# Summing the seven block products of a feed-forward chunk in PSUM instead of on VectorE

## The chip, the core and the metric

The kernel runs on one core of a Trainium2 chip. The metric is the device time of one execution in microseconds (us), as the median of several runs. Of the core's engines the text speaks of TensorE (PE in the profile; its weight loads are PEld), VectorE (DVE), ScalarE (ACT), GpSimd (POOL) and SyncE (SP). SP and POOL issue the DMA transfers that matter here. Matrix products are written to PSUM, which has eight banks of 512 float32 values per partition; DVE and ACT read and write PSUM as well as the main on-chip memory, SBUF.

## The reference: a two-layer decoder trunk

The input `x` is 512 tokens of 1024 channels, float32. Layer 0 mixes tokens by a dilated windowed attention with three head groups, layer 1 by causal pooling over 2, 4, 8 and 16 tokens. Each mixer is followed by the same kind of feed-forward block:

```python
def swiglu_ffn(h, w_gate_up, w_down):
    gu = h @ w_gate_up
    gate, up = gu[..., :D_FF], gu[..., D_FF:]
    return (jax.nn.silu(gate) * up) @ w_down

def reference(x, ...):
    for i in range(DEPTH):            # DEPTH = 2
        x = x + mixer_i(rmsnorm(x, ...))
        x = x + swiglu_ffn(rmsnorm(x, ffn_norm[i]), w_ffn_gate_up[i], w_ffn_down[i])
    return rmsnorm(x, final_norm)
```

`D_FF` is 2816, that is 22 chunks of 128 hidden channels. For one chunk the kernel needs a gate product and an up product of 128 channels each, by 512 tokens, over 1024 input channels.

## The kernel before, in words

**Precision.** Every operand is split into a high part (`hi`, a rounded copy that ACT makes, line 77) and a low part (`lo`, the rest, which DVE makes, line 78). A product is three matmuls, hi by hi, hi by lo and lo by hi, added up in PSUM. The split is done for weights and for activations alike.

**Stages.** Attention comes first (to about 510 us of the span), then layer 0's feed-forward (to about 858), the pooling (to about 918), layer 1's feed-forward, and the final norm in the last few us.

**Order of the feed-forward.** `ffn` handles one layer in two halves of 11 chunks. Chunks 0 to 4 of the first half are done plainly (`plain_pair`): a gate product and an up product of 24 matmuls each with 512 columns. During these, `prepare(k)` builds for k = 0 to 3 the sums and differences of activation blocks, `T`, that the later chunks need. The other 6 chunks of the first half and all 11 of the second go through `strassen_pair`, so there are 17 of them in a layer and 34 in all. After each half come the down products of that half.

**A chunk of seven products.** Gate and up, two halves of the tokens, and two halves of the input channels make a product of 2 by 2 blocks. The kernel forms it from seven block products instead of eight (a Strassen-Winograd scheme). Each block product, `mult`, is 12 matmuls of 256 columns (four k steps of three). `seven` runs them in this order; the weight part (b, s, m or l) and the activation block are in brackets: 11 (b), 21 (b), 1 (s), 3 (s), 2 (m), 22 (m), 4 (l). They go to halves of four PSUM banks, each product into space of its own, and DVE adds them up afterwards: line 412 makes gt from two products and `first`, line 420 makes `sums`, lines 425 and 426 make `up` and the second half of `gt`. ACT copies the first product to SBUF (`first`, line 399), and at the end `activation` does the silu on ACT (line 865), the product of gate and up on DVE (line 866), and the split of the result into hi and lo. The result is written to `act` and feeds the down products. All PSUM tiles come from one ring of eight banks.

**Weights.** A chunk's weights come as `Pair`. `load` issues three DMAs on SP (lines 134, 135 and 136: raw tiles b and a, half tile c) and then one on POOL (line 137), which adds a further block onto b in place while it loads. Four later steps make the split parts: `blocks` (part b, from a), `sums` (part s, from the summed raw tile b), `more` (part m, from a after two additions on DVE, lines 150 and 151) and `last` (part l, from c). The rings are short: five split tiles of type w, two halves, four raw tiles, two raw halves. In program order, `pump` emits the next step as soon as the buffer that it would reuse has been given up (`done()`); `seven` calls `pump` after each product. Counting back five w tiles, part m of the next chunk reuses the tile of part b of this chunk, part b of the chunk after reuses this chunk's s, and part s of the chunk after reuses this chunk's m.

**What sets the order on an engine.** The program is written in one order, but a planner decides, before the kernel runs, the order of the instructions on each engine. It plays the program through with costs of its own and takes, on each engine, the earliest written instruction that is ready at that moment. That order is then fixed. On the chip each engine takes its instructions in it and waits at the first one whose inputs or buffers are not there. Line 77 is the `hi` of a split, line 78 its `lo`, 254, 255 and 257 the matmuls of plain and down products, 371, 372 and 373 those of `mult`.

Of the kernel before, what the change touches and what calls it, by code (L numbers as in the profile page):

```python
# [15 lines left out]
P = 128  # L16
# [32 lines left out]
def trunk(ctx: ExitStack, tc: tile.TileContext, xT, norms, w_first, w_qk, w_qkp, w_v0, w_v0p, w_v12, w_out, w_pair, w_down, w_pin, w_pgrp,  # L49
# [4 lines left out]
    tmp = ctx.enter_context(tc.tile_pool(name="tmp", bufs=2))  # L54
    psum = ctx.enter_context(tc.tile_pool(name="psum", bufs=8, space=PSUM))

# [8 lines left out]

    def ps():
        return psum.tile([P, S], F32, tag="ps", name="ps")

# [157 lines left out]
    class Product:  # L226


        def __init__(self, n, ins, w=None, keep=None):
            self.n, self.ins, self.done, self.p, self.w = n, ins, 0, ps(), w  # L230
            self.sizes = DOWN if n == HALF else (n,)
            self.tiles, self.keep = keep or [], keep is not None
# [133 lines left out]

    def mult(dst, w, half, T, name):
        for k in range(K2):
            c = slice(half * S + k * P, half * S + (k + 1) * P)
            th, tl = T[name, k]  # L370
            nc.tensor.matmul(dst, w.t[0][:, c], th, start=k == 0, stop=False)  # L371
            nc.tensor.matmul(dst, w.t[0][:, c], tl, start=False, stop=False)  # L372
            nc.tensor.matmul(dst, w.t[1][:, c], th, start=False, stop=k == K2 - 1)  # L373

# [53 lines left out]

    def normed(layer, k, row):
# [20 lines left out]

    with tc.tile_pool(name="opool", bufs=1) as opool:
        early = opool.tile([P, HEADS, S], F32R, tag="o", name="early")
# [398 lines left out]

    with tc.tile_pool(name="fpool", bufs=2) as fpool:
        fpool.tile([P, 32], F32, name="shift", bufs=1)
# [9 lines left out]
        def activation(gt, up):  # L863

            nc.scalar.activation(gt, gt, AF.Silu)
            nc.vector.tensor_mul(up, up, gt)
            j = len(act)
            held["a", j], t = slot("a")
            act.append((t[:, 0], t[:, 1]))
            split(*act[-1], up)  # L870

        def unfold(m, p):

            if m == 0:
                held["x", 0], t = slot("xs", F32)
                new = t[:, 0]
            else:
                new = x_tile(m - 1)
            nc.vector.tensor_add(new.rearrange("p (b i r) -> p r i b", r=NT, b=NT), *(
                t.rearrange("p (r i b) -> p r i b", r=NT, b=NT) for t in (X[m], p)))  # L880
            X[m] = new

        def ffn(layer, nxt, lead, row):
# [23 lines left out]
            def prepare(k):  # L907


                h, t = normed(op, k, row)  # L910
                hq, b22 = h.t.rearrange("p (a b c) -> p a b c", a=2, b=2), h.t[:, 3 * H2:]
# [137 lines left out]
        def end(i, half, js, f=None):  # L1049
            f = f or Product(HALF, hidden, keep=ends[i])  # L1050
            return f.add(js, cols=halves[half])

        def add(i, half, f):
            m, cols = KC - 2 + i, halves[half]
            nc.vector.tensor_add(X[m][:, cols], X[m][:, cols], f.p[:, cols])
            sq = ftile("sq", H2)
            nc.scalar.activation(sq, X[m][:, cols], AF.Square)
            return sq
# [106 lines left out]
```

## Time and profile before

| | |
|---|---|
| Timed runs | 1267.69, 1268.29 and 1268.46 us; median 1268.29 us |
| Span of the profiled execution, first to last instruction | 1264.5 us; no other time of that execution is given |
| PE busy | 1250.9 us, 99% of the span |
| DVE busy | 926.3 us, 73% |
| ACT busy | 571.5 us, 45% |
| POOL busy | 130.1 us, 10% |
| Chunks of seven products | 34: starting at 553.7 to 604.4 (6), 674.4 to 775.2 (11), 960.7 to 1011.4 (6) and 1081.3 to 1182.1 us (11) |

The rows of the profile read as follows. A row that groups instructions gives line, engine and operation, then the tiles written and read, the shape, the count, the busy time in us, the mean duration of one in ns, and the idle time of the engine just before these instructions with what ended it. A row of a timeline gives start and duration in us, the engine, the line, and in square brackets the idle time before and its releaser. A row of a stretch gives start and end in us, its length, then the busy time of PE, PEld, DVE, ACT and POOL with the count of instructions, the granted share of the PE clock, the DMA engines' busy share and GB/s. A matmul's duration is longer than the distance to the next one, because matmuls overlap; the distance between starts is what counts.

### The profile page before, as it was taken

The page shows a single profiled execution, that of the slowest core. Times are in us where ns is not written, and L with a number is a line of the kernel's source. Part 1 is how long each engine was busy: PE and PEld are TensorE (multiplying, and loading weights), DVE is VectorE, ACT ScalarE, POOL GpSimd, SP SyncE. Part 2 cuts the span into 40 slices and gives each one's busy share as a digit, 9 for nine tenths or more (in the row PEclk, how much of TensorE's full clock was granted, in tenths as well). Part 3 has the DMA queues.
Part 4 walks back from the last instruction along what each step waited for, and adds up shares of the span by engine and source line. Part 5 has one row for each costly group of instructions (what it writes and reads, how often), then busy time and mean ns, then how long its engine had stood idle before and what let it go on. Part 6 is the DMA issues. An engine that isn't in the chain of part 4 may idle for free.

```text
span 1264.5 us, 21069 instructions
## 1 busy us (share of the span) xinstructions
PE 1250.9 (99%) x8382; PEld 1156.7 (91%) x8382; DVE 926.3 (73%) x1395; ACT 571.5 (45%) x885; POOL 130.1 (10%) x123
## 2 busy tenths in 40 slices
PE   9999999999999999999999999999999999999997
PEld 7889999999999988899989999888789988999987
DVE  6987788878778845689636887558978953788643
ACT  6445554545445543445324554343444532455331
POOL 1011111212111000110001110000301000110000
PEclk9999999999999999999999999999999999999999
DMA  8336556655756433256456774333135645676322
GB/s 295 101 95 164 130 157 145 162 139 144 182 137 152 139 133 120 67 129 181 124 146 158 181 188 126 97 133 130 37 95 123 175 126 142 168 182 173 93 69 67
DMA packets 67875, 174.04 MB, mean 138 GB/s; under 512 B 6960, under 2 KB 9152, under 8 KB 67776
## 3 DMA queue, kind: packets, MB, share of 16 engines
q1 hardware_dynamic: 48816, 136.49, 33.3%
q0 software_dynamic: 17808, 35.14, 16.4%
q8 instruction: 66, 1.08, 0.3%
q10 hardware_dynamic: 1152, 1.05, 0.2%
q14 instruction: 33, 0.27, 0.1%
HBM read 170.56 MB, written 2.10 MB: 137 GB/s over the span
## 4 chain that ended last, share of the span: by engine, by line
PE 75%; issue 12%; DVE 10%; ACT 1%; POOL 1%; DMA 0%; DVEq 0%; POOLq 0%
PE ps L372 13%; PE ps L371 13%; PE ps L373 13%; PE ps L254 8%; PE ps L255 8%; PE ps L257 8%; PE ps L483 2%; PE ps L484 2%; PE ps L485 2%; DVE wlo L78 2%; PE ps L678 1%; PE ps L590 1%; DVE raw L434 1%; POOL rcol L323 1%; PE ps L656 1%
## 5 line engine op out<-in xcount | busy, mean ns | idle before, releaser
L77 ACT ACTIVATE whi<-raw 128x1024 fp32r<-128x1024 f32 (+2 forms) x299 | 298.1, 1002 | 428.2 <-PE ps L255 198.4
L78 DVE TENSOR_TENSOR wlo<-raw,whi 128x1024 fp32r<-128x1024 f32 (+2 forms) x299 | 343.2, 1152 | 158.6 <-ACT whi L77 157.4
L254 PE MATMUL ps<-a,whi 128*128 128x512 f32 (+1 forms) x374 | 141.0, 377 | 0.0
L255 PE MATMUL ps<-a,whi 128*128 128x512 f32 (+1 forms) x374 | 140.9, 377 | 0.0
L257 PE MATMUL ps<-a,wlo 128*128 128x512 f32 (+1 forms) x374 | 140.8, 377 | 0.0
L371 PE MATMUL ps<-tt,whi 128*128 128x256 f32 x408 | 115.5, 283 | 0.0
L372 PE MATMUL ps<-tt,whi 128*128 128x256 f32 x408 | 115.5, 283 | 0.0
L373 PE MATMUL ps<-tt,wlo 128*128 128x256 f32 x408 | 115.5, 283 | 0.0
L137 POOL DMA_DIRECT2D raw<-w_pair x34 | 41.1, 1209 | 440.8 <-DMA raw<-w_pair 152.6
L257 PEld LDWEIGHTS ps<-a,wlo 128*128 128x128 f32 x374 | 70.4, 188 | 13.0
L254 PEld LDWEIGHTS ps<-a,whi 128*128 128x128 f32 x374 | 70.4, 188 | 12.8
L255 PEld LDWEIGHTS ps<-a,whi 128*128 128x128 f32 x374 | 70.4, 188 | 12.7
L371 PEld LDWEIGHTS ps<-tt,whi 128*128 128x128 f32 x408 | 78.3, 192 | 0.0
L372 PEld LDWEIGHTS ps<-tt,whi 128*128 128x128 f32 x408 | 78.3, 192 | 0.0
L373 PEld LDWEIGHTS ps<-tt,wlo 128*128 128x128 f32 x408 | 78.3, 192 | 0.0
L372 PE MATMUL ps<-tb,whi 128*128 128x256 f32 x272 | 77.2, 284 | 0.1
L373 PE MATMUL ps<-tb,wlo 128*128 128x256 f32 x272 | 77.0, 283 | 0.0
L371 PE MATMUL ps<-tb,whi 128*128 128x256 f32 x272 | 76.9, 283 | 0.0
L371 PE MATMUL ps<-h,whi 128*128 128x256 f32 x252 | 72.7, 289 | 0.0
L373 PE MATMUL ps<-h,wlo 128*128 128x256 f32 x252 | 71.3, 283 | 0.0
L372 PE MATMUL ps<-h,whi 128*128 128x256 f32 x252 | 71.3, 283 | 0.0
L254 PE MATMUL ps<-h,whi 128*128 128x512 f32 x144 | 56.4, 392 | 0.0
(280 smaller groups left out, 3415.5 us busy)
## 6 DMA issues: line engine op xcount, KB each, us to landing
raw<-w_pair SPq DMA_DIRECT2D x78, 512.0 KB, 4.3
raw<-w_qkp SPq DMA_DIRECT2D x36, 512.0 KB, 4.7
raw<-w_pair POOLq DMA_DIRECT2D x34, 512.0 KB, 7.2
raw<-w_down SPq DMA_DIRECT2D x32, 384.0 KB, 3.1
raw<-w_down SPq DMA_DIRECT2D x32, 320.0 KB, 2.8
raw<-w_v SPq DMA_DIRECT2D x18, 512.0 KB, 3.9
raw<-w_qkp POOLq DMA_DIRECT2D x18, 512.0 KB, 7.3
rawhalf<-w_pair SPq DMA_DIRECT2D x34, 256.0 KB, 3.5
```

What stands on the lines that cost most here:

```text
L77: nc.scalar.activation(hi, v, AF.Copy)
L78: nc.vector.tensor_tensor(lo, v, hi.bitcast(F32), op=OP.subtract)
L137: nc.gpsimd.dma_start(self.b.t.rearrange("p (a c) -> p a c", a=2), self.src[:, None, 3 * S:].to_broadcast([P, 2, S]), accum_op=OP.add)
L254: nc.tensor.matmul(self.p[:, cols], w[0][:, s], mh[:, cols], start=self.done == 0, stop=False)
L255: nc.tensor.matmul(self.p[:, cols], w[0][:, s], ml[:, cols], start=False, stop=False)
L257: nc.tensor.matmul(self.p[:, cols], w[1][:, s], mh[:, cols], start=False, stop=self.done == self.n)
L371: nc.tensor.matmul(dst, w.t[0][:, c], th, start=k == 0, stop=False)
L372: nc.tensor.matmul(dst, w.t[0][:, c], tl, start=False, stop=False)
L373: nc.tensor.matmul(dst, w.t[1][:, c], th, start=False, stop=k == K2 - 1)
L483: nc.tensor.matmul(o, mh, wh, start=k == 0, stop=False)
L484: nc.tensor.matmul(o, mh, wl, start=False, stop=False)
L485: nc.tensor.matmul(o, ml, wh, start=False, stop=k == K2 - 1)
```

## The change

`strassen_pair` no longer calls `seven`, but a new function, `chain`. The seven products run in another order: 11, 1, 2, 21, 3, 22, 4. Four of them (11, 2, 3, 4) go to the same half bank `c` and add up there, and `c` is read in between:

- after 11, ACT copies `c` to a second bank `d`; after 2, ACT copies `c` to a third bank `e`. Product 21 is then added onto `d`, product 22 onto `e`.
- product 1 has a bank of its own, `a`, and ACT copies it to SBUF (`half`).
- `left`: ACT takes the silu of `d` straight from PSUM into the first half of `gt`. `right`: DVE subtracts `half` from `e`, then ACT takes the silu of that half.
- `high`: DVE subtracts `half` from `c` after product 3 into the second half of `up`. `low`: ACT copies `c` after product 4 into the first half of `up`.

`hide`, the part of `activation` behind the silu, stays: product of gate and up on DVE, then the split. DVE's lines 412, 420, 425 and 426 and ACT's copy `first` are gone from the feed-forward, but not from the attention, which still uses `seven`. The signs are kept right by a flipped sum in `prepare` (`normed(..., flip=True)`), a factor of -1 in the plain chunks' `up`, and a subtraction instead of an addition where the down products are added to `X`. PSUM is no longer one ring of eight in the feed-forward: `c` has 2 banks, `d` and `e` share 3, and `a` and the plain products' ring has 3; whole products alternate between the last two rings.

```diff
+    def banks(stack, **sizes):
+        psum["pool"] = stack.enter_context(tc.tile_pool(name="psum", bufs=1, space=PSUM))
+        psum["sizes"], psum["turn"] = sizes, 0
+
+    def full():
+        tags = [t for t in ("seed", "ps") if t in psum["sizes"]]
+        psum["turn"] += 1
+        return ps(tags[psum["turn"] % len(tags)])
...
-    def mult(dst, w, half, T, name):
+    def mult(dst, w, half, T, name, onto=False):
         for k in range(K2):
             c = slice(half * S + k * P, half * S + (k + 1) * P)
             th, tl = T[name, k]
-            nc.tensor.matmul(dst, w.t[0][:, c], th, start=k == 0, stop=False)
...
+            nc.tensor.matmul(dst, w.t[0][:, c], th, start=k == 0 and not onto, stop=False, skip_group_check=onto)
...
+    def chain(T, share, left, right, low, high):
+        unit, = units.popleft()
+        c, a, d, e = (ps(tag)[:, :H2] for tag in ("sum", "ps", "seed", "seed"))
+        wb = part(unit, "b")
+        mult(c, wb, 0, T, "11")
+        nc.scalar.copy(d, c)
+        pump()
+        ws = part(unit, "s")
+        mult(a, ws, 0, T, "1")
+        share(a)
+        pump()
+        wm = part(unit, "m")
+        mult(c, wm, 0, T, "2", True)
+        nc.scalar.copy(e, c)
+        pump()
+        mult(d, wb, 1, T, "21", True)
+        wb.done()
+        left(d)
+        pump()
+        mult(c, ws, 1, T, "3", True)
+        ws.done()
+        high(c)
+        pump()
+        mult(e, wm, 1, T, "22", True)
+        wm.done()
+        right(e)
+        pump()
+        wl = part(unit, "l")
+        mult(c, wl, 0, T, "4", True)
+        wl.done()
+        low(c)
+        pump()
...
-        nc.vector.tensor_add(t.t[:, 3 * H2:], t.t[:, H2:S], h.t[:, S:3 * H2])
+        if flip:
+            nc.vector.scalar_tensor_tensor(t.t[:, 3 * H2:], t.t[:, H2:S], -1.0, h.t[:, S:3 * H2],
+                                           op0=OP.mult, op1=OP.subtract)
...
+        banks(stack, sum=2, seed=3, ps=3)
...
-                nc.vector.tensor_mul(up, pu, row)
+                nc.vector.scalar_tensor_tensor(up, pu, -1.0, row, op0=OP.mult, op1=OP.mult)
...
             def strassen_pair():
-                gt, up = ftile("gt"), ftile("up")
-                seven(T, gt, up, ftile)
-                activation(gt, up)
+                gt, up, half = ftile("gt"), ftile("up"), ftile("half", H2)
+                lo, hi = slice(0, H2), slice(H2, S)
+
+                def right(p):
+                    nc.vector.tensor_sub(gt[:, hi], p, half)
+                    nc.scalar.activation(gt[:, hi], gt[:, hi], AF.Silu)
+
+                chain(T, lambda p: nc.scalar.copy(half, p),
+                      lambda p: nc.scalar.activation(gt[:, lo], p, AF.Silu), right,
+                      lambda p: nc.scalar.copy(up[:, lo], p),
+                      lambda p: nc.vector.tensor_sub(up[:, hi], p, half))
+                hide(gt, up)
...
-                        nc.vector.tensor_add(X[m], X[m], f.p)
+                        nc.vector.tensor_sub(X[m], X[m], f.p)
...
-            f = f or Product(HALF, hidden, keep=ends[i])
+            f = f or Product(HALF, hidden, keep=ends[i], part=True)
```

More of the change, by code (lines that the diff above doesn't have):

```diff
@@ L54, in trunk @@
     tmp = ctx.enter_context(tc.tile_pool(name="tmp", bufs=2))
-    psum = ctx.enter_context(tc.tile_pool(name="psum", bufs=8, space=PSUM))
+    psum = {}
     def x_tile(k, name="x", dtype=F32):
@@ L64, in trunk, with ps @@
     nhalf = cpool.tile([P, NT], F32, name="nhalf")
[L66 to L67 removed]
+    def ps(tag="ps"):
+        pool, sizes = psum["pool"], psum["sizes"]
+        return pool.tile([P, S], F32, tag=tag, name=tag, bufs=sizes[tag])
+    def banks(stack, **sizes):
[5 more added lines that the diff above has]
+        return ps(tags[psum["turn"] % len(tags)])
     tmp.tile([P, 64], F32, name="shift", bufs=1)
@@ L226, in trunk, with __init__ @@
     class Product:
-        def __init__(self, n, ins, w=None, keep=None):
-            self.n, self.ins, self.done, self.p, self.w = n, ins, 0, ps(), w
+        def __init__(self, n, ins, w=None, keep=None, part=False):
+            self.n, self.ins, self.done, self.w = n, ins, 0, w
+            self.p = ps() if part else full()
             self.sizes = DOWN if n == HALF else (n,)
@@ L370, in mult @@
             th, tl = T[name, k]
-            nc.tensor.matmul(dst, w.t[0][:, c], th, start=k == 0, stop=False)
-            nc.tensor.matmul(dst, w.t[0][:, c], tl, start=False, stop=False)
-            nc.tensor.matmul(dst, w.t[1][:, c], th, start=False, stop=k == K2 - 1)
+            nc.tensor.matmul(dst, w.t[0][:, c], th, start=k == 0 and not onto, stop=False, skip_group_check=onto)
+            nc.tensor.matmul(dst, w.t[0][:, c], tl, start=False, stop=False, skip_group_check=onto)
+            nc.tensor.matmul(dst, w.t[1][:, c], th, start=False, stop=k == K2 - 1, skip_group_check=onto)
     def part(unit, name):
@@ L427, in seven, with normed @@
         behind(6)
-    def normed(layer, k, row):
+    def chain(T, share, left, right, low, high):
[30 more added lines that the diff above has]
+        pump()
+    def normed(layer, k, row, flip=False):
         h, t = Held("raw"), Held("raw")
@@ L448, in in_a_row @@
         return t.rearrange("p (r i b) -> p b i r", b=NT, r=NT)
-    with tc.tile_pool(name="opool", bufs=1) as opool:
+    with tc.tile_pool(name="opool", bufs=1) as opool, ExitStack() as stack:
+        banks(stack, ps=8)
         early = opool.tile([P, HEADS, S], F32R, tag="o", name="early")
@@ L850, in trunk @@
                 note(1, m)
-    with tc.tile_pool(name="fpool", bufs=2) as fpool:
+    with tc.tile_pool(name="fpool", bufs=2) as fpool, ExitStack() as stack:
+        banks(stack, sum=2, seed=3, ps=3)
         fpool.tile([P, 32], F32, name="shift", bufs=1)
@@ L878, in unfold @@
                 new = x_tile(m - 1)
-            nc.vector.tensor_add(new.rearrange("p (b i r) -> p r i b", r=NT, b=NT), *(
+            nc.vector.tensor_sub(new.rearrange("p (b i r) -> p r i b", r=NT, b=NT), *(
                 t.rearrange("p (r i b) -> p r i b", r=NT, b=NT) for t in (X[m], p)))
@@ L907, in prepare @@
             def prepare(k):
-                h, t = normed(op, k, row)
+                h, t = normed(op, k, row, True)
                 hq, b22 = h.t.rearrange("p (a b c) -> p a b c", a=2, b=2), h.t[:, 3 * H2:]
```

6 lines of the change are left out of this document (5 added, 1 removed).

## The prediction

> **What bounds the kernel now.** I read the page first (busy shares and the groups with their idle time), then the four stretches that hold the 34 chunks of seven products, then the waits, and then single timelines inside the chunks.
>
> ```profile
> span 1264.5 us, 21069 instructions
> PE 1250.9 (99%) x8382; PEld 1156.7 (91%) x8382; DVE 926.3 (73%) x1395; ACT 571.5 (45%) x885; POOL 130.1 (10%) x123
> ...
> L371 PE MATMUL ps<-tt,whi 128*128 128x256 f32 x408 | 115.5, 283 | 0.0
> ```
>
> ```profile
> 553.73:614.53 60.80, 60.74 (x506) 60.54 (x505) 53.06 (x77) 31.32 (x46) 4.82 (x4) 1.00 0.66 173
> 674.38:785.26 110.88, 110.88 (x926) 110.87 (x924) 91.60 (x126) 56.20 (x75) 9.66 (x8) 1.00 0.63 166
> 960.69:1021.49 60.80, 60.75 (x506) 60.55 (x505) 52.95 (x77) 31.33 (x46) 4.82 (x4) 1.00 0.64 173
> 1081.33:1192.21 110.88, 110.88 (x926) 110.88 (x925) 90.90 (x125) 55.35 (x74) 9.66 (x8) 1.00 0.61 159
> ```
>
> PE bounds it. The second stretch holds 11 chunks of 84 matmuls in 110.88 us, which is 10.08 us a chunk, 1.44 us a product and 0.12 us a matmul; the fourth is the same to the hundredth. The first and third hold 6 chunks each, 60.48 us at that pace, and take 60.80, so 0.32 us each is lost. That 0.64 us is all the waiting that PE does in the 34 chunks. The change leaves the count and shape of the matmuls alone, so **0.64 us is the most that it can win there**, however much it takes from DVE. What is open is what it loses: today PE runs ahead of DVE and ACT, and from now on it has to wait for them inside a chunk.
>
> How far behind they may be shows here; the last three rows are the second chunk of layer 0's first stretch, from 564.12 on, and the answers below them the second chunk of layer 1's, from 971.06 on.
>
> ```profile
> ACT whi L77 <- DMA raw<-w_pair: 13.1, 5, 5.4
> ```
>
> ```profile
> 563.29 1.06 ACT L77 ACTIVATE whi<-raw 128x1024 fp32r<-128x1024 f32 x1 [1.28 <-DMA raw<-w_pair]
> 568.88 1.06 ACT L77 ACTIVATE whi<-raw 128x1024 fp32r<-128x1024 f32 x1 [4.53 <-DMA raw<-w_pair]
> 569.85 0.62 ACT L77 ACTIVATE halfhi<-rawhalf 128x512 fp32r<-128x512 f32 x1
> 570.37 0.35 ACT L399 COPY first<-ps 128x256 f32<-128x256 f32 x1
> ```
>
> ```profile
> 976.43 1.06 ACT L77 ACTIVATE whi<-raw 128x1024 fp32r<-128x1024 f32 x1 [5.39 <-DMA raw<-w_pair]
> 977.40 0.61 ACT L77 ACTIVATE halfhi<-rawhalf 128x512 fp32r<-128x512 f32 x1
> 977.92 0.35 ACT L399 COPY first<-ps 128x256 f32<-128x256 f32 x1
> ```
>
> ```profile
> 567.00 0.28 PE L371 MATMUL ps<-tt,whi 128*128 128x256 f32 x1
> ```
>
> ```profile
> 973.94 0.28 PE L371 MATMUL ps<-tt,whi 128*128 128x256 f32 x1
> ```
>
> At 568.88 ACT starts the split of part s of the third chunk, after 4.53 us idle for a weight transfer. The copy `first` of the second chunk stands behind that split in ACT's order. Its product ended 1.44 us before 567.00, at 565.56, yet the copy runs at 570.37, 4.8 us late. Layer 1 repeats it at 976.43 with 5.39 us. Today that costs nothing, since PE never waits for `first`.
>
> **The change part by part.** The engines' work, per chunk:
>
> ```profile
> L420 DVE TENSOR_TENSOR sums<-ps,gt 128x512 f32<-128x512 f32 x34 | 23.3, 687 | 4.3 <-PE ps L373 4.1
> L412 DVE TENSOR_TENSOR gt<-ps,first 128x512 f32<-128x512 f32 x34 | 23.3, 685 | 0.0
> L425 DVE TENSOR_TENSOR up<-ps,sums 128x512 f32<-128x512 f32 x34 | 23.3, 685 | 0.0
> ...
> L399 ACT COPY first<-ps 128x256 f32<-128x256 f32 x55 | 20.1, 366 | 29.9 <-PE ps L373 29.9
> L426 DVE TENSOR_TENSOR gt<-sums,ps 128x256 f32<-128x256 f32 x34 | 14.0, 412 | 0.0
> ```
>
> DVE loses 687 + 685 + 685 + 412 = 2469 ns and gains two subtractions of 256 columns, 2 x 412 = 824 (the row of line 426). That is 1.65 us less of the 8.3 us a chunk that the second stretch shows (91.60 / 11). ACT loses `first` (366) and one silu of 512 columns and gains four copies of 256 columns and two silus of 256. I price all six at 366, the copy from PSUM. No row shows a copy into PSUM or a silu out of it; bounds for one are 0.3 (a shorter path) and 0.63 (the 512-column `halfhi` above). The silu taken away is priced at that same 0.63, and ACT ends up about 6 x 0.366 - 0.366 - 0.63 = 1.2 us a chunk busier: 56.20 / 11 + 1.2 = 6.3 of 10.08 us. Both engines keep room, so neither becomes the bound by its total. The flipped sum in `prepare`, the factor -1 and the subtractions from `X` replace one DVE instruction by another of the same shape. They are priced at zero, covered by PE's work, which does not wait for DVE there; without that cover they would cost at most some tenths.
>
> New waits of PE, with products numbered 1 to 7 in the new order: the third (2, onto `c`) must wait until ACT has copied `c` to `d`; the fifth (3) until ACT has copied `c` to `e`; the seventh (4) until DVE has read `c` (`high`). Each has one product, 1.44 us, as cover. Behind each waits the whole rest of PE's stream. How long the read takes in an undisturbed chunk, from ACT's, DVE's and SP's rows:
>
> ```profile
> 723.47 1.06 ACT L77 ACTIVATE whi<-raw 128x1024 fp32r<-128x1024 f32 x1 [1.87 <-PE ps L372]
> ...
> 726.47 0.37 ACT L399 COPY first<-ps 128x256 f32<-128x256 f32 x1 [0.98 <-PE ps L373]
> ...
> 727.74 1.06 ACT L77 ACTIVATE whi<-raw 128x1024 fp32r<-128x1024 f32 x1 [0.35 <-PE ps L372]
> ...
> 730.62 1.06 ACT L77 ACTIVATE whi<-raw 128x1024 fp32r<-128x1024 f32 x1 [1.30 <-PE ps L372]
> ```
>
> ```profile
> 721.63 1.23 DVE L78 TENSOR_TENSOR wlo<-raw,whi 128x1024 fp32r<-128x1024 f32 x1 [1.05 <-ACT whi L77]
> 722.77 0.68 DVE L412 TENSOR_TENSOR gt<-ps,first 128x512 f32<-128x512 f32 x1
> ```
>
> ```profile
> 728.83 1.23 DVE L78 TENSOR_TENSOR wlo<-raw,whi 128x1024 fp32r<-128x1024 f32 x1 [0.31 <-ACT whi L77]
> ```
>
> ```profile
> 730.09 0.33 SPq L135 DMA_DIRECT2D raw<-w_pair  x1
> ```
>
> ```profile
> raw<-w_pair SPq DMA_DIRECT2D x78, 512.0 KB, 4.3
> ```
>
> The chunk starts at 674.38 + 5 x 10.08 = 724.78. Its first product ends at 726.22, the copy runs from 726.47 to 726.84: 0.62 us, and with about 0.1 us to wake PE, 0.7 of 1.44. So in a quiet chunk **both ACT copies are free**; a weight split (1.06) ahead of one makes it at worst 0.3 us late. `high` is tighter. The fifth product of the chunk before ended two products ahead of 724.78, at 721.90, and DVE reads at 722.77, 0.87 us later, because a weight split is in its way. In the new order part m's split falls at the same place (its buffer is freed after the fourth product). With 0.41 for the subtraction and 0.1 to wake PE, 0.87 becomes 1.38 of 1.44. I take zero, and keep the other end for a rival.
>
> The moved splits: part m can begin only after the fourth product instead of the second (727.74 becomes 730.62, where part b's is today) and is needed by the third instead of the fifth. Today it is ready at 728.83 + 1.23 = 730.06, 4.8 us before the next chunk starts and 10.6 us before its use. Minus twice 2.88 leaves 4.8 us. SP's reload of the raw tile a, which waits for that split's end, moves from 730.09 to 732.97 and lands 4.3 later, at 737.3. The split of part b that reads it comes in the next chunk, today at 730.62 + 10.08 = 740.7, then one product later at 742.1, so 4.8 us are left of today's 6.3, and the transfers behind it on SP have no nearer user. Zero for both.
>
> Then **the two late places**. The split of part s keeps its release (after the sixth product of the first chunk, since it reuses part m's buffer in both orders), and the planner evidently thinks the transfer lands well before the second chunk's first product ends: it put both the split and `halfhi` ahead of `first`. I expect the copy to `d` in the same place. What waits behind the split on ACT is then `halfhi`, the right half's silu and the `low` copy of the first chunk, and the copy to `d`; behind that copy stands PE. Layer 0: 569.85 + 0.52 (`halfhi` to the next start) + 3 x 0.366 + 0.1 = 571.57, against 567.00 today: 4.57 us. Layer 1: 977.40 + 0.52 + 1.10 + 0.1 = 979.12 against 973.94: 5.18 us. Sum **9.75 us**. Bounds: directly behind the split, without the other three, 569.85 + 0.47 - 567.00 = 3.32 and 3.93, together 7.3. If the split of the first chunk's result also gets ahead, it adds DVE's multiplication of 512 columns (0.69, as line 420's row) and its own 0.62, 1.3 us at each place: 12.4.
>
> A smaller one is swallowed by this. In the first chunk of a layer, product 1 moves from third to second place (starting 1.44 us earlier), and its last low operand comes late:
>
> ```profile
> 557.14 1.29 DVE L78 TENSOR_TENSOR tt<-raw,tt 128x512 fp32r<-128x512 f32 x2
> ```
>
> The first of the two is done at about 557.8; the matmul that reads it would come at 556.7 (553.73 + 0.32 + 1.44 + 10 x 0.12). That is 1.1 us a layer, but PE waits at 567 for an absolute time in any case, so it only counts where that wait is gone. Later chunks find DVE and ACT caught up, since the data of the following splits have landed by then and DVE has 1.65 us more room in each.
>
> The sum is span 1264.5 + 9.75 = 1274.3; the median of the runs stands 3.8 us above the span, so **1278.0 us**.
>
> **The rivals.** *Not slower: the late places vanish.* If the planner puts the copy to `d` ahead of the waiting split, PE never meets the transfer. Against it: the order above, with the split's release unmoved. For it: the write order of everything around it changes. Left are the 1.1 us a layer, at most 2.2: 1268.3 to 1270.5, 23%, of which I count 17 within 0.2%, the 2.5 us that a measurement of this kernel can tell from no change. It decides as soon as the copy starts before 568.
>
> *Every chunk pays.* If DVE reads for `high` more than 0.93 us after the fifth product (1.44 - 0.41 - 0.1), PE waits each time. With m's split delayed by the `left` silu on ACT (0.366) and still ahead of `high` on DVE, 0.87 becomes 1.24, 0.3 us late, in 34 chunks 10 us on top: 1288. For it: the margin is 0.06 us. Against: a split that late is hardly ready before `high` is. 15%.
>
> *The clock falls in the two gaps.*
>
> ```profile
> 1254.00:1256.00 2.00, 1.38 (x12) 1.21 (x10) 0.85 (x3) 0.42 (x1) 0.00 (x0) 1.00 0.88 291
> 1256.00:1258.00 2.00, 0.90 (x9) 0.90 (x8) 0.31 (x2) 0.00 (x0) 0.70 (x1) 1.00 0.02 8
> 1258.00:1260.00 2.00, 0.26 (x3) 0.07 (x1) 2.00 (x6) 0.38 (x1) 1.24 (x2) 0.54 0.38 127
> ```
>
> At the end, dense work stops shortly after 1254, and the granted clock (the number after POOL's) is 1.00 until 1258 and then 0.54. So about 4 us of thin work ended the full clock. Gaps of 4.6 and 5.2 us could do the same; if the matmuls after each then run at half pace for as long, 4 us of them take 2 us more, 4 us in all: 1282. 12%. The Trainium skill, "TensorE: Matmul & The Clock Gate", Part 1, says that a whole idle window of about 3.4 us halves the clock and that the window runs free; by it a gap of 4.6 us contains a whole window about one time in three, an estimate from that page, and the loss would be some 1.7 us a gap. The 4 us seen here agree with its window.
>
> *Faster* by more than 2.5 us: the stretches give 0.64 at most; only a tail replanned by luck would do it, 4%.
>
> **How the numbers follow.** The forecast itself, 1275.6 to 1280.7 by the bounds of the two places, has 46%; the clock 12%, every chunk 15%, no late place 23%, faster 4%. The likeliest is 1278. The range must reach to the not-slower case and to the case of every chunk, so 1268 to 1290. Slower by over 0.2%: 46 + 12 + 15 + 6 = 79%; same 17%; faster 4%.
>
> **What would show it.** In the new trace PE idles about 4.6 us before the third product of the second chunk in layer 0 and about 5.2 in layer 1, released by ACT's copy to `d`, which stands behind a split that waits for DMA. The long stretches of 11 chunks stay at 110.9 us. DVE's busy time falls by about 34 x 1.65 = 56 us and PE's pace stays at 0.12. Idle of a few tenths in each chunk before the seventh product would speak for the second rival, a granted clock below 1 behind the gaps for the third. I am wrong if there are no two gaps, or if they sit at the fifth or seventh product.

## The result, and the profile after

The changed kernel takes **1283.76 us** (median of 4 runs, 1282.78 to 1284.23) against 1268.1 before: a ratio of **1.0127, 95% interval 1.0114 to 1.0139** (here and below, the ratio is an estimate over the runs, not the quotient of two medians). It is slower, 5.8 us beyond the 1278.0 that was forecast and within the range of 1268 to 1290.

The page of the changed kernel, the span with the busy shares, and the group of products that add onto `c`:

```profile
span 1282.4 us, 21045 instructions
...
PE 1257.0 (98%) x8382; PEld 1160.9 (91%) x8382; DVE 872.8 (68%) x1327; ACT 606.9 (47%) x1021; POOL 130.4 (10%) x123
...
L385 PE MATMUL sum<-tt,whi 128*128 128x256 f32 x272 | 78.5, 289 | 10.5 <-ACT seed L450 10.5
```

DVE gave up 53.5 us and ACT took on 35.4, as intended. The span grew by 17.9 us all the same, and 10.5 us of PE's idle time, none of it there before, stand under one line with one releaser: line 450, the copy to `d`. PE's waits in the changed kernel (line that waits, releaser, us in total, times, longest) show that it is two waits:

```profile
PE sum L385 <- ACT seed L450: 10.5, 2, 5.4
```

ACT's timeline around the two, layer 0 first:

```profile
571.51 1.06 ACT L89 ACTIVATE whi<-raw 128x1024 fp32r<-128x1024 f32 x1 [5.35 <-DMA raw<-w_pair]
572.47 0.40 ACT L993 ACTIVATE gt<-gt 128x256 f32<-128x256 f32 x1
572.78 0.35 ACT L997 COPY up<-sum 128x256 f32<-128x256 f32 x1
573.03 0.63 ACT L89 ACTIVATE halfhi<-rawhalf 128x512 fp32r<-128x512 f32 x1
573.56 0.37 ACT L450 COPY seed<-sum 128x256 f32<-128x256 f32 x1
```

```profile
985.73 1.06 ACT L89 ACTIVATE whi<-raw 128x1024 fp32r<-128x1024 f32 x1 [6.00 <-DMA raw<-w_pair]
...
987.78 0.37 ACT L450 COPY seed<-sum 128x256 f32<-128x256 f32 x1
```

The split of part s stands idle for its transfer, and the right half's silu, the `low` copy, `halfhi` and then the copy to `d` queue behind it. PE's timeline where it goes on in layer 0:

```profile
573.99 0.58 PE L385 MATMUL sum<-tt,whi 128*128 128x256 f32 x1 [5.16 <-ACT seed L450]
574.37 0.42 PE L386 MATMUL sum<-tt,whi 128*128 128x256 f32 x1
574.58 0.41 PE L387 MATMUL sum<-tt,wlo 128*128 128x256 f32 x1
```

The first starts are 0.38 and 0.21 us apart instead of 0.12. The stretches show why (the granted clock is the third number from the end; the first stretch lies inside the wait of layer 0, 574.00 and 988.21 begin what follows the wait in each layer):

```profile
570.77:574.00 3.23, 0.01 (x1) 0.01 (x1) 1.40 (x2) 2.42 (x5) 0.00 (x0) 0.50 0.92 159
574.00:577.60 3.60, 3.60 (x17) 3.60 (x18) 2.83 (x5) 1.25 (x3) 0.00 (x0) 0.50 0.39 115
577.60:579.00 1.40, 1.40 (x13) 1.40 (x13) 0.00 (x0) 0.38 (x1) 0.00 (x0) 1.00 0.92 255
683.05:793.90 110.85, 110.85 (x925) 110.85 (x924) 75.18 (x110) 67.76 (x119) 9.66 (x8) 1.00 0.63 163
...
988.21:994.03 5.82, 5.82 (x27) 5.82 (x28) 2.84 (x5) 1.76 (x4) 0.00 (x0) 0.50 0.47 141
...
1098.24:1209.20 110.96, 110.96 (x925) 110.96 (x924) 74.55 (x105) 67.13 (x118) 9.66 (x8) 1.00 0.62 157
```

The clock was at half behind both waits: 17 matmuls in 3.60 us and 27 in 5.82. At 0.12 each they would take 2.0 and 3.2, so this costs 1.6 + 2.6 = 4.2 us. The two long stretches, 22 of the 34 chunks, are what they were before to a tenth, with 16 us less of DVE in each.

The third loss is far from the chunks. PE's last matmul of the attention and its first of the feed-forward, in the changed kernel; then DVE there:

```profile
497.35 0.39 PE L270 MATMUL ps<-oh,wlo 128*128 128x512 f32 x1
498.62 0.47 PE L267 MATMUL ps<-h,whi 128*128 128x512 f32 x1 [0.87 <-ACT whi L89]
```

```profile
497.78 0.69 DVE L903 TENSOR_TENSOR x<-x,ps 128x512 f32<-128x512 f32 x1 [2.08 <-PE ps L270]
```

The first product of the feed-forward starts 1.27 us after the last matmul ahead of it, instead of the usual 0.23, and 0.15 us after DVE has read the last bank of the attention stage (497.78 + 0.69 = 498.47).

From the distance between the starts of products, the waits are 5.31 us (573.99) and 5.55 us (988.21). With the 4.2 of the clock and about 1.0 at 498 us, 16.1 us of the profile's 17.9 are named, and the ratio of the runs is 16 us too. Most of the rest is 0.5 us in the first 15 us of the program and 0.9 in the last few us.

### The profile page after: what moved, and what is told of

The parts are those of the page before. It is cut to its first block, busy times and chain, and to the rows that moved or that the text cites. A ratio compares the mean times of both kernels' runs of the same rounds, so it can differ in the third digit from the quotient of the medians.

```text
span 1282.4 us, 21045 instructions
## 1 busy us (share of the span) xinstructions
PE 1257.0 (98%) x8382; PEld 1160.9 (91%) x8382; DVE 872.8 (68%) x1327; ACT 606.9 (47%) x1021; POOL 130.4 (10%) x123
## 4 chain that ended last, share of the span: by engine, by line
PE 77%; issue 12%; DVE 5%; DMA 3%; ACT 2%; POOL 1%; SPq 0%; POOLq 0%; DVEq 0%; ACTq 0%
PE ps L267 6%; PE ps L270 6%; PE ps L268 6%; PE ps L385 6%; PE ps L386 6%; PE ps L387 6%; PE sum L385 4%; PE sum L386 4%; PE sum L387 4%; PE seed L267 3%; PE seed L268 3%; PE seed L270 3%; DMA raw<-w_pair 2%; PE seed L385 2%; PE seed L386 2%
## 5 line engine op out<-in xcount | busy, mean ns | idle before, releaser
L385 PE MATMUL sum<-tt,whi 128*128 128x256 f32 x272 | 78.5, 289 | 10.5 <-ACT seed L450 10.5
L386 PE MATMUL sum<-tt,whi 128*128 128x256 f32 x272 | 78.2, 287 | 0.0
L387 PE MATMUL sum<-tt,wlo 128*128 128x256 f32 x272 | 78.1, 287 | 0.0
L267 PE MATMUL ps<-a,whi 128*128 128x512 f32 (+1 forms) x209 | 76.8, 368 | 0.0
L268 PE MATMUL ps<-a,whi 128*128 128x512 f32 (+1 forms) x209 | 76.7, 367 | 0.0
L270 PE MATMUL ps<-a,wlo 128*128 128x512 f32 (+1 forms) x209 | 76.6, 367 | 0.0
L267 PE MATMUL seed<-a,whi 128*128 128x512 f32 x165 | 64.2, 389 | 0.0
L268 PE MATMUL seed<-a,whi 128*128 128x512 f32 x165 | 64.2, 389 | 0.0
L270 PE MATMUL seed<-a,wlo 128*128 128x512 f32 x165 | 64.2, 389 | 0.0
L385 PEld LDWEIGHTS sum<-tt,whi 128*128 128x128 f32 x272 | 53.4, 196 | 11.0 <-ACT seed L450 11.0
L386 PEld LDWEIGHTS sum<-tt,whi 128*128 128x128 f32 x272 | 53.5, 197 | 0.0
L387 PEld LDWEIGHTS sum<-tt,wlo 128*128 128x128 f32 x272 | 53.4, 196 | 0.0
L386 PEld LDWEIGHTS ps<-h,whi 128*128 128x128 f32 x252 | 48.3, 192 | 0.0
L385 PEld LDWEIGHTS ps<-h,whi 128*128 128x128 f32 x252 | 48.3, 192 | 0.0
L387 PEld LDWEIGHTS ps<-h,wlo 128*128 128x128 f32 x252 | 48.2, 191 | 0.0
```

What stands on the lines that cost most here:

```text
L267: nc.tensor.matmul(self.p[:, cols], w[0][:, s], mh[:, cols], start=self.done == 0, stop=False)
L268: nc.tensor.matmul(self.p[:, cols], w[0][:, s], ml[:, cols], start=False, stop=False)
L270: nc.tensor.matmul(self.p[:, cols], w[1][:, s], mh[:, cols], start=False, stop=self.done == self.n)
L385: nc.tensor.matmul(dst, w.t[0][:, c], th, start=k == 0 and not onto, stop=False, skip_group_check=onto)
```

## The experiments

The cuts of code below are shortened; `...` marks what is left out, and comments behind `#` are added for the reader.

**Without the adding transfer.** Theory: what costs is a late transfer with PE's copy behind it in ACT's fixed order. Then PE waits no longer when the transfer is early. POOL's transfer, which adds a block onto part s's raw tile in place and so lands last, is left out in the feed-forward, so the output is another one and 512 KB less are moved in each chunk; the work of PE, ACT and DVE stays.

```diff
-            nc.gpsimd.dma_start(self.b.t..., accum_op=OP.add)
+            if self.add:          # False for the feed-forward's pairs
+                nc.gpsimd.dma_start(self.b.t..., accum_op=OP.add)
```

> The changed kernel without the adding transfer on POOL for the chunks of the feed-forward: part s is made of the raw tile as it was loaded, so one block is left out of a sum and the output is another; the work of PE, ACT and DVE and their order stay. The late tile is there some 6 us earlier. My theory: ACT's split no longer waits and both gaps go with the order of the copies unchanged, clock 1.00; about 1270 us. Rival (order of products, or the copies themselves): about 1284.

Measured: 1268.62 us, ratio 1.0008 (0.9999 to 1.0018). ACT's timeline in layer 0's second chunk, in the order of the changed kernel but for `halfhi`, which now stands ahead of the `low` copy:

```profile
565.66 2.01 ACT L89 ACTIVATE whi<-raw 128x1024 fp32r<-128x1024 f32 x2 [2.25 <-PE sum L390]
567.58 0.40 ACT L997 ACTIVATE gt<-gt 128x256 f32<-128x256 f32 x1
567.88 0.62 ACT L89 ACTIVATE halfhi<-rawhalf 128x512 fp32r<-128x512 f32 x1
568.41 0.35 ACT L1001 COPY up<-sum 128x256 f32<-128x256 f32 x1
568.66 0.37 ACT L454 COPY seed<-sum 128x256 f32<-128x256 f32 x1
```

The same pieces of work stand ahead of the copy (the first row holds two splits), but none waits for a transfer, and the copy comes at 568.66 instead of 573.56. Almost the whole loss is gone (1.0008 instead of 1.0127), with the copies, the adding up in one bank and the two pools still in place. In its waits line 450 (454 here) is left with 0.5 us, once.

**The copy ahead of the late split.** The same theory, from the other side: the transfer stays late, but part s's split is put behind the copy to `d` in the second chunk of each layer.

```diff
-        nc.scalar.copy(d, c)
+        copied = nc.scalar.copy(d, c)
+        if at == 1:                       # second chunk of a layer
+            with tc.issue_after(copied.ins):
+                pump()
         pump()
...
         low(c)
-        pump()
+        if at != 0:                       # the first chunk leaves that step to the second
+            pump()
```

> The changed kernel, but in the second chunk of each layer the late split of part s is put behind the copy of c to d in ACT's order (its emission is moved, and an order is given for ACT alone). Nothing else is moved. My theory (a copy that stands behind a split waiting for a transfer): the gaps before the third product go; the split still stands ahead of the copy to e, so PE now waits before the fifth product, about 2.2 us in layer 0 and 2.5 in layer 1, too short for the clock to fall. Time about 1274 us, granted clock 1.00 over all chunks. Rival (the new order of products needs its weight parts too early, or copies into PSUM are dear): nothing changes, about 1284.

Measured: 1274.33 us, ratio 1.0052 (1.0037 to 1.0067). Its waits, and the stretches around the new wait in layer 0:

```profile
PE sum L385 <- ACT seed L461: 2.4, 2, 1.9
```

```profile
570.56:573.97 3.41, 1.51 (x14) 1.31 (x12) 2.19 (x3) 2.23 (x5) 0.00 (x0) 1.00 0.95 199
573.97:577.38 3.41, 3.41 (x16) 3.41 (x17) 2.55 (x4) 1.89 (x3) 0.00 (x0) 0.50 0.77 203
```

The third product waits no more. The fifth does, on the copy to `e`, which now stands behind the split: 2.06 us in layer 0, 0.64 in layer 1. The time was as expected, but by luck: 4.7 us of waiting at the full clock were expected, and 2.7 us came, with about 1.5 us on top from 16 matmuls at half clock. The clock fell after a wait of only 2.06 us. The last section returns to this.

**Behind the copy to `e` as well.** The split goes one copy further down; the second chunk's pumps ahead of this place are dropped.

```diff
-        nc.scalar.copy(e, c)
+        copied = nc.scalar.copy(e, c)
+        if at == 1:
+            with tc.issue_after(copied.ins):
+                pump()
         pump()
```

> As the run before, but the split is put behind the copy of c to e as well. My theory: no wait of PE on either copy; what is left is DVE's read of c before the seventh product, behind the two late splits, about 0.8 us in layer 0 and 1.0 in layer 1. Time about 1271 us: 1268.1, 1.1 where the second PSUM pool is opened at 497 us, and 1.8. Rival (weight parts, or dear copies): about 1284.

Measured: 1273.25 us, ratio 1.0042 (1.0027 to 1.0057). Its waits:

```profile
PE sum L385 <- DVE up L1004: 3.0, 2, 1.6
```

The wait is now at the seventh product, released by `high` (line 1004 here): DVE stands in the `lo` parts of the late splits. It is 1.58 and 1.73 us between starts, about twice the 0.8 and 1.0 expected, which is most of why the time is 1273 and not 1271; the clock stayed at full. So each of the three reads that PE waits for inherits the same late transfer in turn.

**Keeping PE busy in the two waits.** This prices the clock by itself: 11 float32 matmuls of 256 columns into a spare bank, whose result nobody reads, ahead of the third product of the two chunks.

```diff
+        count.append(1)
+        if len(count) in (2, 19):         # second chunk of each layer
+            fill = ps("ps")
+            for i in range(11):
+                nc.tensor.matmul(fill[:, :H2], X[0][:, :P], X[0][:, :H2], start=True, stop=True)
```

> The changed kernel with 11 float32 matmuls of 256 columns added in the two gaps (second chunk of each layer, before the third product), into a bank that nobody reads: about 4.7 us of work for PE at full clock, no longer than the gaps. It tells the gap from the clock. If half of the loss behind the gaps is the clock: the third product starts at the same moment as before (within 0.5 us), the clock stays at 1.00, and the time falls by the 1.7 and 2.6 us that the halved clock cost in the profile, to about 1279.5. If the clock cost nothing: 1283.8, the same as the changed kernel.

Measured: 1279.05 us, ratio 1.0088 (1.0071 to 1.0105). The stretches behind the two places:

```profile
574.00:577.00 3.00, 3.00 (x28) 3.00 (x27) 2.39 (x4) 1.65 (x4) 0.00 (x0) 1.00 0.42 121
987.00:990.00 3.00, 3.00 (x27) 3.00 (x26) 1.79 (x3) 1.67 (x5) 0.00 (x0) 1.00 0.65 183
```

The third product still starts when the copy lets it (573.54 in layer 0 against 573.99), but runs at the full clock. The changed kernel is 1283.76 - 1279.05 = 4.7 us longer. Some 0.5 us of that need not be the clock: in the two profiles the changed kernel is that much later before the feed-forward begins. From the third product of layer 0's second chunk to that of layer 1's it takes 414.22 us instead of 412.41, and from there to PE's end 2.6 us more. That is 4.4 us for the clock by this run, beside 4.2 counted in the trace.

**Two pools, alone.** The kernel before, with its ring of eight banks opened a second time where the feed-forward begins.

```diff
     with tc.tile_pool(name="fpool", bufs=2) as fpool, ExitStack() as stack:
+        banks(stack)                      # again eight banks, one ring
```

> The kernel before, with one thing of the change alone: the eight banks of PSUM are opened as two pools, one for the stages up to the attention's end and one for the rest, still one ring of eight in each. Theory (the first product of the feed-forward stage now waits until VectorE has read the last bank of the old pool): 1.1 us at about 497 us, so a ratio of 1.0009 and PE starting that stage near 498.6 instead of 497.1; nothing else moves. Rival (the 1.1 us came from the planner's order or from chance): 1268.1 within 0.4 us, the stage starting near 497.1.

Measured: 1268.25 us, ratio 1.0007 (0.9998 to 1.0016). The time alone doesn't tell the two theories apart; PE's timeline does:

```profile
497.02 0.39 PE L260 MATMUL ps<-oh,wlo 128*128 128x512 f32 x1
498.28 0.47 PE L257 MATMUL ps<-h,whi 128*128 128x512 f32 x1 [0.87 <-ACT whi L80]
```

The same hole, 1.26 us between the starts, in a kernel without any other part of the change. The releaser that the profile names, a weight split, can hardly be the cause, since the kernel before has it at the same place while PE is already at work (ACT and PE there):

```profile
497.03 1.07 ACT L77 ACTIVATE whi<-raw 128x1024 fp32r<-128x1024 f32 x1 [3.24 <-PE ps L255]
```

```profile
497.06 0.39 PE L254 MATMUL ps<-h,whi 128*128 128x512 f32 x1
```

That split ends at 498.10, a microsecond after the product started. What is left is DVE's last read of the old pool, whose end lies 0.14 us ahead of PE's start here too (497.45 + 0.69 = 498.14); it is the reading that fits, not one that a run has separated from the split. That the second pool brings the hole is shown from both sides: the changed kernel with one ring, below, has none there (its first product starts 0.23 us behind the last one ahead of it).

**The order of the products, alone.** The kernel before, four banks and DVE's additions kept, with the order 11, 1, 2, 21, 3, 22, 4.

```diff
-                seven(T, gt, up, ftile)
+                reordered(T, gt, up, ftile)   # mult in the new order, the same additions
```

> The kernel before, with four banks of its own for each chunk and the additions on VectorE as they were, but with the products in the changed kernel's order (11, 1, 2, 21, 3, 22, 4) and the weight parts released as there. Theory (what costs is that PE waits on copies inside a chunk, while the order by itself costs nothing, since PE reads no copy here): the late copy stays late and nobody waits for it; 1268 within 2 us, no gap over 1 us in the 34 chunks, the clock at 1.00. Rival (the new order brings the weight parts too late): slower by over 5 us, gaps of PE released by a split of a weight part.

Measured: 1269.04 us, ratio 1.0010 (1.0001 to 1.0019). Its waits on `mult`:

```profile
PE ps L373 <- DVE wlo L78: 1.2, 2, 0.8
```

PE waits 0.8 and 0.4 us for a late `lo` part of a weight in the third chunks, so the rival of late weights is real but small. The split of part s is as late as ever, and nobody waits for the copy behind it.

**One ring of eight for the changed kernel.**

```diff
-        c, a, d, e = (ps(tag)[:, :H2] for tag in ("sum", "ps", "seed", "seed"))
+        c, a, d, e = (ps()[:, :H2] for i in range(4))
...
-        banks(stack, sum=2, seed=3, ps=3)
```

> The changed kernel with one ring of eight banks for the whole program; the four banks of a chunk come from it in turn, products and copies as in the change. Theory (the second pool costs 1.1 us once, the two gaps and the clock behind them the rest): 1282.6 us, so about 1.1 below the changed kernel; gaps of 5.3 and 5.6 us at the same two products, the clock at 0.50 behind them. Rival (the split of the banks into rings of 2, 3 and 3 is what makes products wait): the gaps shrink or go, 1273 or less.

Measured: 1279.38 us, ratio 1.0096 (1.0083 to 1.0110), some 3 us less than expected. Its waits, and the stretches behind the two:

```profile
PE ps L385 <- ACT ps L450: 8.5, 2, 4.7
...
PE ps L386 <- DVE tt L90: 0.9, 2, 0.5
```

```profile
571.98:575.39 3.41, 2.91 (x13) 2.91 (x14) 3.36 (x6) 1.34 (x4) 0.00 (x0) 0.50 0.20 58
984.99:988.40 3.41, 2.93 (x13) 2.93 (x14) 3.34 (x6) 1.32 (x4) 0.00 (x0) 0.50 0.50 114
```

The two waits stay at the same products, so the division of the banks isn't their cause. They are shorter, 8.5 instead of 10.5 in total; between starts 4.90 instead of 5.31 us in layer 0 and 3.90 instead of 5.55 in layer 1. Two things add up there. The wait for `T` in the first chunks came back (0.9 us in total, 0.6 us a layer between starts), and PE arrives that much later at the copy. And in layer 1 the split began 8.8 us behind the issue of the adding transfer instead of 9.7, in layer 0 9.7 instead of 9.5; why, no run shows. The clock stayed down for one stretch of 3.41 us a layer instead of two.

**Both splits late, one ring.** What remains if all three reads are put ahead of the late splits in the second chunk?

```diff
         read = high(c)
+        if at == 1:                       # the four pumps ahead of this are dropped there
+            with tc.issue_after(copied.ins), tc.issue_after(read.ins):   # copy to e, high
+                pump(2)
```

> The changed kernel with one ring of eight banks and, in the second chunk of each layer alone, the splits of the third chunk's parts s and m put behind that chunk's copy to e on ScalarE and behind its read of c (high) on VectorE. Theory (nothing but the three reads that stand behind a waiting split cost time, and the pool): both gaps go, the clock stays at 1.00, the 11 chunks of a long stretch take 110.9; 1268.5 us, between 1267.5 and 1270.5, no faster than the kernel before, since PE had only 0.64 us to win. Rival (the splits are then late for the third chunk): a gap of 1 to 3 us moves there, 1271 to 1274.

Measured: 1274.21 us, ratio 1.0048 (1.0034 to 1.0062): the rival, at the upper end of its range. The second chunk has no wait left; the third has one. ACT's timeline there:

```profile
577.15 2.94 ACT L89 ACTIVATE whi<-raw 128x1024 fp32r<-128x1024 f32 x3
579.99 0.62 ACT L89 ACTIVATE a<-up 128x512 fp32r<-128x512 f32 x1
580.51 0.37 ACT L450 COPY ps<-ps 128x256 f32<-128x256 f32 x1
```

Three splits in a row, put off from the second chunk, stand ahead of the third chunk's copy to `d`. PE waits 1.93 us for it in each layer.

**The third chunk mended too.**

```diff
+        if at == 2:                       # third chunk
+            with tc.issue_after(first.ins):   # first = the copy to d
+                pump(2)
...
-        pump()
+        if at != 1:                       # the second chunk: none behind the sixth and seventh product
+            pump()
```

> The kernel of e9_best with the third chunk mended too: in the second chunk no further splits are put out after those of parts s and m, and in the third chunk two splits stand behind its copy to d, so that one split instead of three, and the split of the hidden activation, stand ahead of that copy on ScalarE. In e9_best three splits of 0.98 us each stood there and PE waited 1.93 us a layer. Theory (each wait is just what stands ahead of the copy): two splits fewer take 2 us off, the 1.93 us go to zero, 0.6 us a layer stays in the first chunk for its late operand: 1274.2 - 3.9 = 1270.3 us or somewhat less, between 1268.0 and 1271.5. Rival (the work only slides on): a wait of 1 to 2 us turns up at the third chunk's copy to e or in the fourth chunk, 1272.5 to 1274.5.

Measured: 1271.59 us, ratio 1.0037 (1.0023 to 1.0050). Its waits:

```profile
PE ps L385 <- ACT ps L450: 1.1, 2, 0.6
PE ps L386 <- DVE tt L90: 0.9, 2, 0.5
```

The wait went on to the fourth chunk's copy to `d`, down to 0.78 and 0.63 us between starts. The time lies between the two ranges that were written down, 0.1 us above the theory's. The theory was right on the third chunk's copy, and the rival right that the backlog slides on, though by less than it said. No version beats the kernel before.

## Why the prediction was right, and where it was not

That 1283.76 lies within the range proves little, since the range is 22 us wide. What speaks for the prediction is the mechanism: the two places, the product, the releaser and the work ahead of the copy on ACT came out as written. The number 1278.0 was missed by 5.8 us. Three terms make that up: the clock (4.2), the size of the two waits (1.1) and the second pool (1.0), together 6.3.

**The bound** held. PE sets the end, the long stretches keep 110.85 and 110.96 us, and taking 53.5 us (56 forecast) from DVE won nothing.

**The two late places** held, with the work ahead of the copy on ACT that was written down: the split, `halfhi`, and the silu and the `low` copy of the chunk before (`halfhi` came last of them). The runs without the adding transfer and with the copy ahead of the split show that this is the cause. **The term's size** was off: 5.31 + 5.55 = 10.9 us instead of 9.75. The step took the transfer's landing from the old trace. Counted from the start of the second chunk (PE's first matmul of it), the split began 568.88 - 564.12 = 4.8 us in before and 571.51 - 565.79 = 5.7 after. In layer 1 it is 976.43 - 971.06 = 5.4 before and 985.73 - 979.78 = 6.0 after. That is 1.0 and 0.6 us later; what lay behind the split took 0.2 less a place than priced, since the silu and the `low` copy are followed 0.31 and 0.25 us behind their starts, not 0.366.

POOL's rows show more of the delay. In layer 0 the adding transfer was issued at 562.03 in before and at 562.05 after, which is 1.65 us earlier counted from the chunk, and yet the split began 6.9 us behind that issue in before and 9.5 after; in layer 1 it is 9.1 and 9.7. The fast one of the four was issued 2.4 us behind the plain load that SP had issued last (559.66), the others 0.6 to 0.8 us behind theirs. In the runs with the order alone and with one ring, with 0.6 to 0.9 us, it is 8.8 to 9.7 too. This fits two transfers that share the DMA engines, but no run separates it. The share of the engines' busy time hardly tells the kernels apart: 92% in the stretch in which it ran, and 90% in the same stretch of before (563.33 to 569.10). The changed kernel there:

```profile
565.00:570.77 5.77, 3.83 (x32) 3.63 (x31) 1.42 (x2) 1.06 (x1) 1.20 (x1) 1.00 0.92 237
```

**The clock**, held at 12%, did fall in both places. Its price was forecast at 4 us and came out at 4.2 in the trace and 4.4 to 4.7 by the run that keeps PE busy. This is the step that failed: the likeliest case was taken with the clock at full, though its own waits of 4.6 and 5.2 us were as long as the thin stretch that ended the full clock in the quoted rows. The Trainium skill, "TensorE: Matmul & The Clock Gate", Part 1, asks for a whole idle window of about 3.4 us. The trace disagrees on that point, with a fall after 2.06 us. The trace of before disagreed already: its clock fell at about 1258.2, and in the 3.41 us ahead of that PE was busy for 1.69 us.

**The second pool** was not priced at all: 1.0 us at 498 us, shown in the trace of the run that has nothing else of the change.

**`T` of the first chunk** (1.1 us a layer if uncovered) was called swallowed. In the changed kernel it doesn't show, and not because a wait behind it swallowed it: the planner put ten matmuls of the third product and the first of the fourth ahead of the last two of the second product, which read the late operand and so start at 559.67 without a wait. It shows with one ring, at about half the size: 0.6 us a layer between starts. There it is swallowed in the wait behind it, as said.

**Every chunk pays** was wrong by the margin that was written down. DVE in a quiet chunk, which starts at 723.43 and ends its fifth product at 723.43 + 5 x 1.44 = 730.63:

```profile
730.36 1.22 DVE L90 TENSOR_TENSOR wlo<-raw,whi 128x1024 fp32r<-128x1024 f32 x1 [2.93 <-ACT whi L89]
731.50 0.42 DVE L998 TENSOR_TENSOR up<-sum,half 128x256 f32<-128x256 f32 x1
```

`high` starts 0.87 us after the product, the number taken over from the old trace, and ends at 731.92, 0.14 us ahead of the seventh product at 732.06. In the run with the split behind both copies this read comes later still, and there the margin fails (1.58 and 1.73 us).

**ACT's price** held: 35.4 / 34 = 1.04 us a chunk, against 1.2. The copy into PSUM, which no row of before showed:

```profile
L450 ACT COPY seed<-sum 128x256 f32<-128x256 f32 x34 | 12.2, 359 | 15.7 <-PE sum L387 15.7
L997 ACT COPY up<-sum 128x256 f32<-128x256 f32 x34 | 12.1, 355 | 0.6 <-PE sum L387 0.6
```

359 ns, as long as one out of it, and 366 was taken.

**The base** was a little off too. The forecast added 3.8 us between span and median; the profiled execution of the changed kernel took 1284.18 us, 1.8 above its span. If that holds before, the profiled execution of before took some 2 us less than the median of its runs, and the terms are to be added to the median.

## What to carry to other kernels

Work taken off an engine that isn't the bound was worth nothing here (53.5 us of DVE), and a read inside the chain of the engine that is the bound turns a delay in the reader's queue, beyond its cover of one product, into a delay of the end; so look, before such a change, at what stands ahead of the new read on its engine, above all a load that waits for a transfer. Price such a wait at its latest landing, not at the old trace's. A short hole can cost most of itself a second time through the clock (2.06 us of waiting were followed by 16 matmuls in 3.41 us, 1.5 us more than at full pace), so price the clock into every wait of a PE that is otherwise dense.

## What the hardware showed that was not expected

The clock doesn't need one long hole. In each kernel whose clock fell in the chunks, falls and returns lie a whole number of steps of 3.41 us apart (the two falls of the changed kernel, at 570.77 and 987.20, 122 steps of 3.413). Taken on that raster, these are the windows of 3.41 us around the waits: the changed kernel in layer 0 and, behind its wait, layer 1; then the run with both copies ahead of the split (PE's busy time is the second number):

```profile
567.36:570.77 3.41, 1.47 (x13) 1.27 (x11) 0.06 (x1) 0.00 (x0) 1.20 (x1) 1.00 0.93 247
570.77:574.18 3.41, 0.19 (x1) 0.20 (x2) 1.58 (x2) 2.42 (x5) 0.00 (x0) 0.50 0.88 151
...
987.20:990.61 3.41, 2.40 (x11) 2.40 (x12) 3.41 (x6) 1.85 (x5) 0.00 (x0) 0.50 0.37 68
990.61:994.03 3.42, 3.42 (x18) 3.42 (x18) 0.44 (x1) 0.87 (x2) 0.00 (x0) 0.50 0.69 219
```

```profile
572.74:576.15 3.41, 1.99 (x18) 1.79 (x16) 3.41 (x6) 2.28 (x3) 0.00 (x0) 1.00 0.68 129
```

```profile
982.34:985.75 3.41, 1.84 (x16) 1.64 (x15) 3.41 (x5) 2.35 (x4) 0.00 (x0) 1.00 0.80 180
```

A window with PE busy for 1.47 us (43%) was followed by half clock, as was the one with 1.51 (44%) in the run with the copy to `d` ahead of the split. Windows with 1.99 (58%) and, in layer 1 of the run with both copies ahead, 1.84 (54%) were not; there the clock stayed full. On the way back, a window at half clock with 2.40 us (70%) was followed by another at half clock, and one with 2.91 (85%), in the run with one ring, by the full clock. So in the chunks the busy share of a window goes with what the clock does next, with a bound between 44% and 54% on the way down, and on the way up between 70% and 85%.

The end of the program doesn't fit this at first sight. In the run that fills the waits, this is the last window ahead of its only fall:

```profile
1265.16:1268.57 3.41, 2.38 (x20) 2.21 (x19) 2.02 (x6) 0.42 (x1) 0.06 (x1) 1.00 0.81 269
```

It shows 70% and was followed by half clock; the last windows of the other kernels, with 45 to 63%, were too. What sets them apart is the matmuls of a single column for the final norm, four or eight of them in each window; a group of four counts as busy for 0.50 or 0.61 us. Without them this window has 42% and the others less, and the bound holds. Leaving them out was decided after the fact, so this is a reading that fits, not a test.

Whether one lost window or two follows should then depend on where the wait falls in the raster. That fits the one ring, which lost one window a layer where the changed kernel lost two. The rule is read from these few windows, and matmul ends are modelled, so the bounds are rough; no run moved a wait of one length across the raster to test it.

The other surprise is the second pool of banks: it cost 1.0 us, where one ring went on without a pause. Its first product seems to have waited until the old pool's last bank was read.
